# A layer norm whose mean and 1/std are read by VectorE straight from one double PSUM bank, and a last norm whose second half is summed earlier

## The chip, the cores and the metric

The kernel runs on one core of one Trainium2 chip. The metric is the device time of one execution in microseconds (us); the figure that counts is the median of several runs. A core has five engines that run their own queues in order: TensorE (PE; its weight loads are listed as PEld), VectorE (DVE), ScalarE (ACT), GpSimd (POOL) and SyncE (SP), which here only issues DMA transfers. PSUM is the memory that TensorE writes its products to; SBUF is the working memory of all engines.

## The reference: what is computed

Two layers of an encoder work on 576 tokens together: 512 of a prompt and 64 of a running stream with caches. Each layer ends in two residual sums with a layer norm behind each:

```python
mix = jnp.concatenate([conv_out, attn_out], axis=-1) @ w_o
x = layer_norm(ALPHA * x + mix, ln1_g, ln1_b)
gate, up = jnp.split(x @ w_gate_up, 2, axis=-1)
ffn = (jax.nn.silu(gate) * up) @ w_down
x = layer_norm(ALPHA * x + ffn, ln2_g, ln2_b)
```

Here `layer_norm` takes mean and variance over the 1024 features of a token. So there are four such norms: after `w_o` and after `w_down` in layer 0, and the same two in layer 1. The last of them gives the output `y`.

## The kernel before

**Layout.** The features lie on the partitions: X is held as 8 blocks (`KD` = 8) of 128 features by 576 tokens, in fp32. The tokens are worked on in two halves of 288 (`H[0]`, `H[1]`, `HT` = 288). Each matrix product is made of three fp32r products, with every operand split into a high part (XH, whi, hh; written by ScalarE) and a low part (XL, wlo, hl; the difference, written by VectorE or GpSimd).

**Order of the work.** The program records every operation with a priority (`nc.prio`, set locally by `with at(...)`) and a planner then places them on the engines one by one, by its own costs, by the priorities and by when buffers come free. That is why all operations carry one line number in the profile, L362, where the planner issues them. A buffer that is used in turn (`IN_TURN`) passes to its next user when its last reader is planned. The pool `pw` has one such buffer, tag "w": two PSUM banks of 512 fp32 columns, which the function `wide` hands out. The stats, the spreads, the convolution and others all take it in turn.

**A norm.** `residual` makes the product that is added to X, one block m of 128 features after the other: five blocks one by one, then the last three (m = 5, 6, 7) together, first the three of token half 0, then the three of half 1 (`order="last"`). For each block and half `take` adds the product to X (VectorE, "X<-X,prod") and `Sums.add` adds x and x squared to the running sums s1 and s2: ScalarE squares (tile sq), GpSimd adds, and VectorE adds for the very last block (`eng`, argument `last`). When block 7 of a half is summed, `Sums.norm` runs for that half:

- `Moments.stats`: six small matmuls with a column of ones give the sums over the partitions (tile stats, in the wide buffer), then six small operations on 96 x 3 numbers (five on VectorE, the square root on ScalarE) give minus mean and 1/std (tile st).
- `Moments.spread(0)` and `spread(1)`: three matmuls each against the identity bring minus mean, then 1/std, to all 128 partitions (tile spread, in the wide buffer), and ScalarE copies each to SBUF (tiles nmu and rstd). The second spread needs the wide buffer that the first copy frees.
- For the 8 blocks: add nmu, multiply by rstd (VectorE, "X<-X,nmu" and "X<-X,rstd"), gain and offset (ScalarE, "X<-X,prm"), and then XH (ScalarE) and XL (VectorE) for the next products; in the last norm a DMA to `y` instead.

The priorities of half 0's last takes and norm lie below those of half 1 by 300, so half 0's norm comes first.

Of the kernel before, what the change touches and what calls it, by code (L numbers as in the profile page):

```python
# [17 lines left out]
P = 128  # L18
D = 1024
KD = D // P  # L20
# [3 lines left out]
HT = T // 2  # L24
# [341 lines left out]
def stream_step(ctx, tc, ins, outs):  # L366
    ctx.enter_context(tc.nc.allow_low_precision(reason="float32r parts"))
    nc = Plan(tc)
# [16 lines left out]
    ident = const.tile([P, P], F32, name="ident")  # L385
# [4 lines left out]
    H = (slice(0, HT), slice(HT, T))  # L390
# [12 lines left out]
    def f(x):  # L403
        return x.bitcast(F32)
# [3 lines left out]
    def bank(name, tag="b"):  # L408
        return pb.tile([P, 512], F32, tag=tag, name=name, bufs=BANKS[tag])

    def wide(name):
        return pw.tile([P, 2, 512], F32, tag="w", name=name)
# [8 lines left out]
    def tmp(name, tag, n=T, bufs=2):  # L421
        return work.tile([P, n], F32, tag=tag, name=name, bufs=bufs)

    def probs(name):
        return tmp(name, "r", T, 3)
# [17 lines left out]
    def weight(src, n):  # L443

        raw = wp.tile([P, KD * P], F32, tag="raw", name="raw", bufs=2)
        hi = wp.tile([P, KD * P], F32R, tag="whi", name="whi")
        lo = wp.tile([P, KD * P], F32R, tag="wlo", name="wlo")
        nc.sync.dma_start(raw[:, :n], src)
        nc.scalar.activation(hi[:, :n], raw[:, :n], AF.Copy)
        nc.either.tensor_sub(lo[:, :n], raw[:, :n], f(hi[:, :n]))  # L450
        return hi, lo
# [74 lines left out]
    class Sums:  # L526
# [2 lines left out]
            self.s1 = slot.tile([P, UW], F32, tag="u0", name="s1")[:, :T]  # L529
            self.s2 = slot.tile([P, UW], F32, tag="u1", name="s2")[:, :T]  # L530

        def add(self, m, h, last=False):
            x = X[:, m, H[h]]
            a, b = self.s1[:, H[h]], self.s2[:, H[h]]
            if m == 0:
                ps = bank("shift")
                nc.tensor.matmul(ps[:, :HT], ones, x, start=True, stop=True)
                nc.vector.scalar_tensor_tensor(x, ps[:, :HT], -1.0 / P, x, op0=OP.mult, op1=OP.add)
                if h == 0:
                    self.c = slot.tile([P, UW], F32, tag="u2", name="shift")[:, :T]  # L540
                nc.scalar.activation(self.c[:, H[h]], ps[:, :HT], AF.Copy, scale=-1.0 / P)
                nc.gpsimd.tensor_copy(a, x)
                nc.scalar.activation(b, x, AF.Square)
                return
            eng = nc.vector if last else nc.gpsimd
            sq = probs("sq")[:, :HT]
            nc.scalar.activation(sq, x, AF.Square)
            eng.tensor_add(a, a, x)
            eng.tensor_add(b, b, sq)

        def norm(self, prm, og, ob, h, last):
            x = lambda k: X[:, k, H[h]]
            nmu, rstd = dst = [tmp(x, x, HT, n) for x, n in (("nmu", 1), ("rstd", 2))]
            mo = Moments(self.s1[:, H[h]], self.s2[:, H[h]], D, HT, 3, dst)
            mo.stats()
            mo.spread(0)
            mo.spread(1)
            for k in range(KD):
                nc.vector.tensor_add(x(k), x(k), nmu)
                nc.vector.tensor_mul(x(k), x(k), rstd)  # L560
                nc.scalar.activation(x(k), x(k), AF.Identity, scale=prm[:, og + k:og + k + 1],
                                     bias=prm[:, ob + k:ob + k + 1])
                if last:
                    nc.sync.dma_start(outs["y"][:, k, H[h]], x(k))
                else:
                    nc.scalar.activation(XH[:, k, H[h]], x(k), AF.Copy)
                    nc.vector.tensor_sub(XL[:, k, H[h]], x(k), f(XH[:, k, H[h]]))

    def residual(prm, wsrc, nk, rhs, og, ob, alpha, last=False):

        s = Sums()

        def take(m, h, ps):
            x = X[:, m, H[h]]
            if m == 0:
                nc.vector.scalar_tensor_tensor(x, x, alpha, ps[:, :HT], op0=OP.mult, op1=OP.add)
            else:
                nc.vector.scalar_tensor_tensor(x, x, alpha, s.c[:, H[h]], op0=OP.mult, op1=OP.add)
                nc.vector.tensor_add(x, x, ps[:, :HT])
            s.add(m, h, m == KD - 1)  # L580

        for m in range(KD - 3):
            out = products([weight(wsrc[m], nk * P)], rhs)[0]
            for h in range(2):
                take(m, h, out[h])
        ws = [weight(wsrc[m], nk * P) for m in range(KD - 3, KD)]
        urgent = nc.prio - 3000
        warm = small.tile([P, 1], F32, tag="warm", name="warm", bufs=2)
        for k in (nk // 2 - 1, nk - 1):
            nc.scalar.activation(warm, f(rhs[k][0][:, T - 1:T]), AF.Sqrt, bias=ones[:, 0:1], scale=0.0)  # L590

        def finish(i, h, ps):
            with at(urgent + 300 * h + 50 * i):
                take(KD - 3 + i, h, ps)
                if i == 2:
                    s.norm(prm, og, ob, h, last)

        products(ws, rhs, "last", take=finish)
# [728 lines left out]
```

## Time and profile before

| | |
|---|---|
| runs, us | 1522.31, 1516.83, 1520.78 (median 1520.78) |
| the profiled execution, us | 1524.12, with a span of 1522.4 from first to last instruction |
| mean granted TensorE clock | 0.939 of full speed |
| busy, share of the span | PE 95%, PEld 93%, DVE 73%, ACT 47%, POOL 33% |
| the chain that ended last | PE 78%, DVE 13%, ACT 3%, issue 2%, DMA 2% |

Busy times are sums over stages with different limits. In the product stages TensorE is at 100%; a norm is a place where the others decide when TensorE goes on. [...]

### The profile page before, as it was taken

How to read it: one execution, taken by the hardware profiler on the slowest of the kernel's cores; microseconds unless marked ns; L12 is line 12 of the kernel's file. 1: busy time of each engine (PE TensorE's matmuls, PEld its weight loads, DVE VectorE, ACT ScalarE, POOL GpSimd, SP SyncE). 2: the span in 40 equal slices, each digit the busy share in tenths (PEclk: the TensorE clock that was granted, in tenths of full speed). 3: DMA queues.
4: the chain of work that ended last, by engine and by line, in shares of the span. 5: the costliest groups of instructions: out<-in, count | busy, mean ns of one | idle time of the engine just before them, and what ended most of it. 6: DMA issues, size and time to landing. Idle time of an engine off the chain costs nothing.

```text
span 1522.4 us, 26598 instructions
## 1 busy us (share of the span) xinstructions
PE 1449.1 (95%) x10246; PEld 1413.3 (93%) x10246; DVE 1104.6 (73%) x2040; ACT 721.4 (47%) x1421; POOL 496.0 (33%) x437
## 2 busy tenths in 40 slices
PE   6999999998999999999998998999899999999996
PEld 6889897997999999999998998889889999999996
DVE  3679886468678577587768997855596875865875
ACT  4444445645446245265444434465363552543643
POOL 2322554243113123033614245633420230320342
PEclk9989787898999999999999995959999999999997
DMA  5614220011222322223234241101112222222221
GB/s 201 188 52 119 54 70 17 29 56 56 77 104 78 103 89 92 84 98 103 69 102 125 86 125 52 45 14 42 56 50 88 99 94 87 94 91 81 80 74 63
DMA packets 66207, 125.12 MB, mean 82 GB/s; under 512 B 27936, under 2 KB 34208, under 8 KB 66080
## 3 DMA queue, kind: packets, MB, share of 16 engines
q1 hardware_dynamic: 66080, 123.42, 25.3%
q8 instruction: 80, 1.31, 0.4%
q14 instruction: 47, 0.39, 0.1%
HBM read 108.81 MB, written 9.21 MB: 78 GB/s over the span
## 4 chain that ended last, share of the span: by engine, by line
PE 78%; DVE 13%; ACT 3%; issue 2%; DMA 2%; POOL 1%; SPq 1%; ACTq 0%; DVEq 0%; POOLq 0%
PE prod L362 33%; PE q L362 16%; PE r L362 8%; PE conv L362 5%; PE c L362 4%; PE po L362 3%; DVE X L362 2%; DVE sel L362 2%; DVE rope_h L362 2%; PE qk L362 2%; PE dots L362 2%; PE pp L362 2%; PE spread L362 2%; DVE wlo L362 2%; PE stats L362 1%
## 5 line engine op out<-in xcount | busy, mean ns | idle before, releaser
L362 DVE TENSOR_TENSOR wlo<-raw,whi 128x512 fp32r<-128x512 f32 (+2 forms) x199 | 246.2, 1239 | 90.8 <-ACT whi L362 88.7
L362 ACT ACTIVATE whi<-raw 128x1024 fp32r<-128x1024 f32 (+2 forms) x206 | 182.9, 889 | 254.5 <-PE prod L362 179.1
L362 PE MATMUL prod<-XH,whi 128*128 128x288 f32 (+2 forms) x928 | 282.9, 310 | 18.5 <-ACT whi L362 16.4
L362 PE MATMUL prod<-XH,wlo 128*128 128x288 f32 (+2 forms) x928 | 285.0, 310 | 7.4 <-DVE wlo L362 7.4
L362 PE MATMUL prod<-XL,whi 128*128 128x288 f32 (+2 forms) x928 | 285.9, 310 | 2.9 <-DVE XL L362 2.8
L362 PE MATMUL prod<-hl,whi 128*128 128x288 f32 x704 | 208.1, 296 | 0.7 <-DVE hl L362 0.5
L362 PE MATMUL prod<-hh,wlo 128*128 128x288 f32 x704 | 207.8, 296 | 0.0
L362 PE MATMUL prod<-hh,whi 128*128 128x288 f32 x704 | 207.0, 295 | 0.0
L362 PEld LDWEIGHTS prod<-XH,whi 128*128 128x128 f32 (+1 forms) x928 | 177.6, 193 | 22.5 <-ACT whi L362 17.3
L362 PEld LDWEIGHTS prod<-XH,wlo 128*128 128x128 f32 (+1 forms) x928 | 177.9, 192 | 10.4 <-DVE wlo L362 8.3
L362 PEld LDWEIGHTS prod<-XL,whi 128*128 128x128 f32 (+1 forms) x928 | 178.9, 193 | 7.7 <-DVE XL L362 5.8
L362 ACT ACTIVATE whi<-s 128x512 fp32r<-128x512 f32 x160 | 96.4, 626 | 134.9 <-PE q L362 102.0
L362 DVE TENSOR_TENSOR wlo<-s,whi 128x512 fp32r<-128x512 f32 x158 | 107.7, 703 | 63.5 <-ACT whi L362 62.5
L362 PE MATMUL q<-XH,wlo 128*128 128x288 f32 x480 | 141.2, 296 | 1.5 <-DVE wlo L362 1.3
L362 PE MATMUL q<-XL,whi 128*128 128x288 f32 x480 | 141.4, 295 | 0.0
L362 PE MATMUL q<-XH,whi 128*128 128x288 f32 x480 | 141.3, 295 | 0.0
L362 PEld LDWEIGHTS prod<-hl,whi 128*128 128x128 f32 x704 | 132.1, 188 | 1.8 <-DVE hl L362 1.4
L362 PEld LDWEIGHTS prod<-hh,wlo 128*128 128x128 f32 x704 | 132.0, 188 | 0.1
L362 PEld LDWEIGHTS prod<-hh,whi 128*128 128x128 f32 x704 | 131.9, 188 | 0.2
L362 POOL TENSOR_TENSOR s<-raw 128x512 f32<-128x512 f32 x28 | 45.0, 1611 | 247.8 <-DVE wlo L362 209.7
L362 DVE TENSOR_TENSOR X<-X,prod 128x288 f32<-128x288 f32 x120 | 53.4, 451 | 86.8 <-PE prod L362 86.1
L362 POOL TENSOR_TENSOR taps<-eyes,wv 128x640 f32<-128x640 f32 x64 | 86.9, 1361 | 71.0 <-PE conv L362 57.2
(197 smaller groups left out, 3560.1 us busy)
## 6 DMA issues: line engine op xcount, KB each, us to landing
raw<-in_w_u SPq DMA_DIRECT2D x44, 512.0 KB, 3.2
raw<-in_w_g SPq DMA_DIRECT2D x44, 512.0 KB, 3.2
raw<-in_w_in SPq DMA_DIRECT2D x36, 512.0 KB, 3.9
raw<-in_w_d SPq DMA_DIRECT2D x48, 384.0 KB, 3.0
raw<-in_w_o SPq DMA_DIRECT2D x16, 512.0 KB, 3.3
raw<-in_w_d SPq DMA_DIRECT2D x16, 256.0 KB, 2.6
rope_s<-rope_h SPq DMA_DIRECT2D x48, 72.0 KB, 2.0
ud<-u SPq DMA_DIRECT2D x8, 320.0 KB, 2.9
```

The costliest lines, as they stand in the source:

```text
L362: getattr(engine, op.method)(*map(take, op.args), **{k: take(v) for k, v in op.kw.items()})
```

## The change

`norm` no longer copies: both spreads go into one wide buffer, minus mean into bank 0 and 1/std into bank 1, and VectorE's adds and multiplications read them there. The buffer is held until half 0's last multiplication. `norm` gets a priority of its own, 125 above that of the half's takes. In the last norm alone, the takes of half 1 get the priority of those of half 0, ahead of half 0's norm, and block 6 of half 1 is summed by VectorE too.

```diff
-        def add(self, m, h, last=False):
+        def add(self, m, h, by_vector=False):
...
-            eng = nc.vector if last else nc.gpsimd
+            eng = nc.vector if by_vector else nc.gpsimd
...
         def norm(self, prm, og, ob, h, last):
             x = lambda k: X[:, k, H[h]]
-            nmu, rstd = dst = [tmp(x, x, HT, n) for x, n in (("nmu", 1), ("rstd", 2))]
-            mo = Moments(self.s1[:, H[h]], self.s2[:, H[h]], D, HT, 3, dst)
+            mo = Moments(self.s1[:, H[h]], self.s2[:, H[h]], D, HT, 3, None)
             mo.stats()
-            mo.spread(0)
-            mo.spread(1)
+            ps = wide("spread")
+            for b in range(2):
+                for i in range(3):
+                    nc.tensor.matmul(ps[:, b, i * mo.m:(i + 1) * mo.m],
+                                     mo.st[:mo.m, b, i:i + 1].to_broadcast([mo.m, P]), ident[:mo.m, :mo.m],
+                                     start=True, stop=True)
+            nmu, rstd = ps[:, 0, :HT], ps[:, 1, :HT]
...
-            s.add(m, h, m == KD - 1)
+            s.add(m, h, m >= KD - 1 - (last and h))
...
-            with at(urgent + 300 * h + 50 * i):
+            with at(urgent + (-300 if last else 300) * h + 50 * i):
                 take(KD - 3 + i, h, ps)
+            with at(urgent + 300 * h + 125):
                 if i == 2:
                     s.norm(prm, og, ob, h, last)
```

The planner makes an order of its own from this. The rows below are of the built programs; "waits" names the engines whose semaphores the instruction waits for, and a row with xN stands for N equal instructions.

TensorE, last norm, half 0, before: from the first spread to the second (spread writes minus mean, then 1/std; prod is block 5 of half 1).

```order
L362 MATMUL spread<-ident,st 128x96 [waits DVE_49]
L362 MATMUL spread<-ident,st 128x96 x2
L362 MATMUL prod<-hh_15247,whi 128x288
L362 MATMUL prod<-hl_15261,whi 128x288
L362 MATMUL prod<-hh_15247,wlo 128x288
L362 MATMUL prod<-hh_15386,whi 128x288
L362 MATMUL prod<-hl_15400,whi 128x288
L362 MATMUL prod<-hh_15386,wlo 128x288
L362 MATMUL spread<-ident,st 128x96 [waits DVE_49,Activation_49]
L362 MATMUL spread<-ident,st 128x96 x2
```

The same place in the changed program.

```order
L362 MATMUL spread<-ident,st 128x96 [waits DVE_49]
L362 MATMUL spread<-ident,st 128x96 x2
L362 MATMUL prod<-hh_15217,whi 128x288
L362 MATMUL prod<-hl_15231,whi 128x288
L362 MATMUL prod<-hh_15217,wlo 128x288
L362 MATMUL spread<-ident,st 128x96 [waits DVE_49]
L362 MATMUL spread<-ident,st 128x96
L362 MATMUL spread<-ident,st 128x96 [waits DVE_49]
L362 MATMUL prod<-hh_15356,whi 128x288
```

Three products fewer stand between the spreads, and the second spread is cut: it has a wait for VectorE ahead of its first and ahead of its third matmul.

VectorE, last norm, half 0's norm and what follows to half 1's stats, before (X<-X,prod are the takes of half 1's blocks 6 and 7, s_15953 and s_15951 its s1 and s2).

```order
L362 TENSOR_TENSOR X<-X,nmu 128x288 [waits Activation_49]
L362 TENSOR_TENSOR X<-X,nmu 128x288 x3
L362 TENSOR_TENSOR X<-X,rstd 128x288 [waits DVE_49,Activation_49]
L362 TENSOR_TENSOR X<-X,rstd 128x288 [waits DVE_49] x3
L362 TENSOR_TENSOR X<-X,nmu 128x288 x2
L362 TENSOR_TENSOR X<-X,rstd 128x288 [waits DVE_49] x2
L362 TENSOR_TENSOR X<-X,prod 128x288 [waits PE_49] x2
L362 TENSOR_TENSOR s_15953<-s_15953,X 128x288 [waits DVE_49,Pool_49]
L362 TENSOR_TENSOR s_15951<-s_15951,sq 128x288 [waits Activation_49,Pool_49]
L362 TENSOR_SCALAR st<-stats 96x3 [waits PE_49]
```

(The pair of rows for two adds and two multiplications stands twice in the program.) The same place in the changed program; the spread operand is minus mean or 1/std.

```order
L362 TENSOR_TENSOR X<-X,spread 128x288 [waits PE_49] x3
L362 TENSOR_TENSOR X<-X,spread 128x288 [waits DVE_49] x3
L362 TENSOR_TENSOR X<-X,spread 128x288 x2
L362 TENSOR_TENSOR X<-X,prod 128x288 [waits PE_49]
L362 TENSOR_TENSOR X<-X,spread 128x288 [waits DVE_49]
L362 TENSOR_TENSOR s_15923<-s_15923,X 128x288 [waits DVE_49,Pool_49]
L362 TENSOR_TENSOR s_15921<-s_15921,sq 128x288 [waits Activation_49,Pool_49]
L362 TENSOR_TENSOR X<-X,spread 128x288 x2
L362 TENSOR_TENSOR X<-X,prod 128x288 [waits PE_49]
L362 TENSOR_TENSOR s_15923<-s_15923,X 128x288 [waits DVE_49]
L362 TENSOR_TENSOR X<-X,spread 128x288 [waits DVE_49] x2
L362 TENSOR_SCALAR st<-stats 96x3 [waits PE_49]
```

(Three rows of the same kinds are left out ahead of the last two.) The first three adds each wait for TensorE; half 1's takes and sums now stand between half 0's adds and multiplications, and the last multiplications of half 0 come right ahead of half 1's statistics, whose first matmul on TensorE waits for them.

TensorE, norm after `w_o` of layer 0, half 1, in the changed program, from the first spread on (prod is now the first product of the feed-forward part).

```order
L362 MATMUL prod<-XL,whi 128x288
L362 MATMUL spread<-ident,st 128x96 [waits DVE_49,PE_49]
L362 MATMUL spread<-ident,st 128x96 x2
L362 MATMUL prod<-XH,wlo 128x288
L362 MATMUL spread<-ident,st 128x96 [waits DVE_49] x2
L362 MATMUL spread<-ident,st 128x96
```

Before, six products stood between the two spreads of that half; here it is one, and the second spread waits for VectorE ahead of its first and its second matmul. In layer 1 the attention's and the convolution's instructions also stand in another order, on all engines: a planner that works from start to end carries any difference on. On TensorE 623 of 9559 instructions stand in other places by a comparison of the two orders, most of them between layer 0's last norm and layer 1's attention.

## Rows read from the trace of the kernel before

**Rows 1.** The profile's page: busy time of each engine, and the granted clock in 40 slices of the span.

```profile
PE 1449.1 (95%) x10246; PEld 1413.3 (93%) x10246; DVE 1104.6 (73%) x2040; ACT 721.4 (47%) x1421; POOL 496.0 (33%) x437
PEclk9989787898999999999999995959999999999997
```

**Rows 2.** The timeline of the last norm from 1497.4 us, VectorE: start, duration, operation, count, idle time before it and what ended it.

```profile
1496.98 0.45 DVE L362 TENSOR_TENSOR X<-X,prod 128x288 f32<-128x288 f32 x1 [0.28 <-PE prod L362]
1498.07 2.28 DVE L362 TENSOR_TENSOR X<-X,nmu 128x288 f32<-128x288 f32 x4 [0.55 <-ACT nmu L362]
...
1503.96 0.82 DVE L362 TENSOR_TENSOR X<-X,rstd 128x288 f32<-128x288 f32 x2
1504.70 0.81 DVE L362 TENSOR_TENSOR X<-X,prod 128x288 f32<-128x288 f32 x2
1506.12 1.05 DVE L362 TENSOR_TENSOR s<-s,X 128x288 f32<-128x288 f32 x1 [0.61 <-POOL s L362]
...
1512.16 1.56 DVE L362 TENSOR_TENSOR X<-X,nmu 128x288 f32<-128x288 f32 x4 [1.55 <-ACT nmu L362]
1514.26 1.56 DVE L362 TENSOR_TENSOR X<-X,rstd 128x288 f32<-128x288 f32 x4 [0.53 <-ACT rstd L362]
...
1517.94 0.83 DVE L362 TENSOR_TENSOR X<-X,rstd 128x288 f32<-128x288 f32 x2
```

**Rows 3.** The same stretch on TensorE and ScalarE: the spreads and their copies in half 0, the last product, and half 1's stats and spreads (a matmul of fp32 is two passes, so x6 are three).

```profile
1496.78 0.81 PE L362 MATMUL spread<-ident,st 96*128 96x96 f32 x6
1497.63 0.41 ACT L362 ACTIVATE nmu<-spread 128x288 f32<-128x288 f32 x1 [0.69 <-PE spread L362]
1498.25 0.81 PE L362 MATMUL spread<-ident,st 96*128 96x96 f32 x6
1502.78 0.29 PE L362 MATMUL prod<-hh,wlo 128*128 128x288 f32 x1
1507.32 1.09 PE L362 MATMUL stats<-ones,s 128*96 128x1 f32 x6 [4.25 <-DVE s L362]
1508.66 1.12 PE L362 MATMUL stats<-ones,s 128*96 128x1 f32 x6 [0.25 <-DVE st L362]
1510.03 1.59 PE L362 MATMUL spread<-ident,st 96*128 96x96 f32 x6 [0.25 <-DVE st L362]
1512.18 1.59 PE L362 MATMUL spread<-ident,st 96*128 96x96 f32 x6 [0.56 <-ACT nmu L362]
1518.44 1.14 ACT L362 ACTIVATE X<-X,prm 128x288 f32<-128x288 f32 x2 [0.33 <-DVE X L362]
```

**Rows 4.** All instructions that write X on VectorE: duration in ns, least/median/most.

```profile
L362 DVE TENSOR_TENSOR X<-X,prod x120: 438/454/464, 293.9 to 1505.1; 128x288 f32<-128x288 f32 x120
L362 DVE TENSOR_TENSOR X<-X,nmu x64: 445/454/1052, 335.0 to 1517.6; 128x288 f32<-128x288 f32 x64
L362 DVE TENSOR_TENSOR X<-X,rstd x64: 445/454/485, 336.8 to 1518.3; 128x288 f32<-128x288 f32 x64
```

**Rows 5.** ScalarE's copies of a spread: duration in ns, least/median/most, of all eight halves.

```profile
L362 ACT ACTIVATE nmu<-spread x8: 388/412/413, 334.5 to 1511.7; 128x288 f32<-128x288 f32 x8
```

**Rows 6.** TensorE's idle times of 0.25 us or more in and behind the norms after `w_o` (layer 0, then layer 1), from its timeline.

```profile
346.19 0.61 PE L362 MATMUL prod<-XH,wlo 128*128 128x288 f32 x1 [3.55 <-DVE wlo L362]
348.00 1.09 PE L362 MATMUL stats<-ones,s 128*96 128x1 f32 x6 [0.48 <-DVE s L362]
368.97 0.40 PE L362 MATMUL prod<-XL,whi 128*128 128x288 f32 x1 [0.56 <-DVE XL L362]
...
1094.92 0.40 PE L362 MATMUL prod<-XH,wlo 128*128 128x288 f32 x1 [3.55 <-DVE wlo L362]
1117.71 0.40 PE L362 MATMUL prod<-XL,whi 128*128 128x288 f32 x1 [0.56 <-DVE XL L362]
```

**Rows 7.** Windows around those two idle times and around the last norm, and around a stall in layer 1's attention: length, TensorE's busy time and instructions, granted clock, DMA.

```profile
346.00:359.00 13.00, 12.33 (x55) 0.50 0.22 82
1096.00:1106.00 10.00, 9.26 (x44) 0.52 0.27 101
1503.00:1506.00 3.00, 0.08 (x1) 0.99 0.70 231
1506.00:1510.00 4.00, 2.21 (x12) 0.50 0.21 69
917.00:944.00 27.00, 25.01 (x117) 0.50 0.14 41
```

**Rows 8.** TensorE's timeline in the norm after `w_down` of layer 0: the spreads, and the idle times beside them.

```profile
751.62 0.81 PE L362 MATMUL spread<-ident,st 96*128 96x96 f32 x6
755.72 0.67 PE L362 MATMUL prod<-XH,whi 128*128 128x288 f32 x3 [0.87 <-ACT XH L362]
768.27 0.81 PE L362 MATMUL spread<-ident,st 96*128 96x96 f32 x6
```

**Rows 9.** TensorE's longest idle time in layer 1's attention.

```profile
916.30 0.66 PE L362 MATMUL qk<-k,q 128*128 128x128 f32 x2 [3.48 <-DVE mx L362]
```

## The prediction

> **What bounds the kernel now.** I read the page first: TensorE is busy for 95% of the span, VectorE for 73%, ScalarE for 47% [rows 1]. So work taken off ScalarE or VectorE is worth something only where TensorE stands still, and the row of granted clocks has three dents beside its end [rows 1]. The places that the change touches were then read from TensorE's timeline and from windows around its idle times. The last norm [rows 2, 3]: half 0's first spread ends at 1496.78 + 0.81 = 1497.59, ScalarE copies it from 1497.63, VectorE adds from 1498.07. The last product ends at 1502.78 + 0.29 = 1503.07, and TensorE then waits 4.25 us until half 1's sums are there (1507.32). From there nothing covers anything: stats, spread, copy, adds, spread, copy, multiplications, each behind the one before, all at a granted clock of 0.50 [rows 7], and the last multiplication ends at 1517.94 + 0.83 = 1518.77. The norms behind `w_o` each hold an idle time of 3.55 us that VectorE's wlo ends, and shorter ones [rows 6]; behind the long one the clock stands at 0.50 or 0.52 for 13 and 10 us [rows 7]. In the norm behind layer 0's `w_down` the only idle time near the spreads is 0.87 us [rows 8].
>
> **What is removed.** Sixteen copies on ScalarE, 412 ns each [rows 5], are 6.6 us of an engine that is busy for half of the span: nothing by itself. What counts is the delay of one copy ahead of the first add (1497.63 to 1498.07, 0.44 us), and of a second ahead of the multiplications in half 1. If only this happened, half 0 of the last norm would begin 0.44 us earlier and half 1 would end 2 x 0.44 = 0.9 us earlier.
>
> **What VectorE pays for reading PSUM.** The trace has that very shape: X plus a product in PSUM takes 438/454/464 ns (120 of them), X plus nmu in SBUF 445/454/1052, X times rstd 445/454/485 [rows 4]. Same median. So 128 operations cost between 128 x (438 - 454) = -2.0 us and 128 x (464 - 454) = +1.3 us of VectorE's time, and I take nothing. A small gain speaks from the one slow group: the first four adds of half 0 took 2.28 us where four others took 1.56 [rows 2], so that 0.7 us hung on something that readers of SBUF met there; adds that read PSUM may lose it. [...]
>
> **The hidden wait.** The wide buffer is one tile, and the built program orders its users as a whole: a matmul that writes bank 1 waits for an add that only reads bank 0, and the next add waits for that matmul. This is to be seen in the rows of order in the section on the change. In half 0 the order becomes add 0, two matmuls of the second spread, add 1, the third matmul, add 2. In half 1 (and where the first matmul goes ahead of add 0) it is add 0, two matmuls, add 1. TensorE works in order, so it stands still behind each such wait, and every product behind it too.
>
> **Last norm, half 0.** A release takes about 0.04 us (1497.59 to 1497.63), a matmul of a spread 0.81 / 3 = 0.27 at full clock [rows 3], a VectorE operation 0.45, and in a row one each (1.56 - 0.45) / 3 = 0.37 [rows 2]. Add 0 from 1497.63 to 1498.08; two matmuls to 1498.66; add 1 from 1498.70 to 1499.15; third matmul to 1499.46; add 2 from 1499.50. The 0.44 that the copy gave back is gone by then, and more. Up to half 0's last multiplication there are 22 VectorE operations (16 of the norm, two takes, four sums, two of these formerly GpSimd's); 20 from add 2 on are 19 x 0.37 + 0.45 = 7.48, to 1506.98. The 0.61 us that VectorE waited for GpSimd's sum [rows 2] goes. Stats need the buffer, free at 1506.98, and begin some 0.15 later, as before behind the sum (1506.12 + 1.05 to 1507.32): 1507.13, or 0.2 earlier. TensorE loses about 0.20 ahead of the second spread (three products end at 1497.59 + 0.33, add 0 at 1498.08 and a release) and 0.53 ahead of its third matmul: the last product ends near 1503.8. This is hidden, as VectorE reaches block 7's take about 1505.
>
> **Last norm, half 1.** Stats to first spread took 1510.03 - 1507.32 = 2.71 [rows 3], so it runs from 1509.84 to 1511.43 (1.59). First matmul of the second, 1.59 / 3 = 0.53, to 1511.96; add 0 to 1512.45; two matmuls to 1513.55; add 1 from 1513.59; 15 operations, 14 x 0.37 + 0.45 = 5.63, to 1519.22. That is +0.45 against 1518.77; ScalarE's gain and the output's transfer follow as before (rows 3's last). In half 1 the copies' 0.9 us are paid back by matmuls that now stand ahead of add 1. I take **+0.5**. [...] Upper bound: sums that wait for a square or a take, +1.3.
>
> **Norms behind `w_o`.** TensorE's two new waits (0.2 + 0.53) fall into the time before 346.19 and 1094.92, and shorten the 3.55 us there, as the end of that is set by VectorE's queue: half 0's norm, then XL, then wlo. That queue loses the waits ahead of add 1 and add 2 (1498.70 - 1498.08 and 1499.50 - 1499.15: 0.62 + 0.35 us) and gains the 0.44 of the copy and up to 0.7 of the slow adds: wlo comes between 0.2 earlier and 0.5 later. In half 1 TensorE has one new wait of about 0.55 (add 0 and two releases), and the norm starts earlier against the idle of 0.56 before an XL [rows 6], which may take part of it. I take **+0.5** for each of the two, with -0.6 and +1.3 as ends.
>
> **Norm behind layer 0's `w_down`.** No long idle time covers it. New waits of 0.73 in half 0 and 0.55 in half 1, 1.3 in all, against 0.87 us of idle time [rows 8] that they may fall into: between 0.4 and 1.3, I take **+0.8**.
>
> **The rest of the order.** Layer 1's attention and convolution come out in another order, since their pieces are planned among the changed norms. Their cost can't be summed. The nearest rows: a stall of 3.48 us behind VectorE's mx [rows 9], and the 27 us at a clock of 0.50 behind it, with 25 us of TensorE's work in them [rows 7], which at full clock would be half, some 12.5 less. Such a place may vanish or another may arise; I take **0**, and -4 to +4 for small shifts.
>
> **Sum.** 0.5 + 2 x 0.5 + 0.8 + 0 = +2.3 with all taken at their middle; the possible shortening of the slow adds in four half 0s is worth some 0.5 less where it lies on a path, which makes +1.8. The profiled execution took 1524.12, so 1525.9 for such a one; it stands 3.3 above the runs' median of 1520.78, against which the forecast is **1522.5**. I count 0.5%, 7.6 us, as the least that a measurement of this kernel can tell: below 1513.2 is faster, above 1528.4 slower.
>
> **Rivals.**
> 1. *The change does only what it says.* If the waits on the whole tile fall where the engines wait anyway, the last norm gives 0.44 + 0.9 less, four other halves up to 0.44 each: -1 to -5, **1518**. For it: the removed idle on GpSimd. Against: the order of VectorE's first adds shows the waits. Chance 0.18.
> 2. *A half-clock stretch goes, faster.* If TensorE's idle time of 3.55 us shrinks enough for the clock to stay at 1.00, the 13 us at 0.50 and 10 us at 0.52 [rows 7] give back up to 12.33 / 2 + 9.26 / 2 = 10.8 us; or the 27 us of layer 1's attention give 12.5. One of them: **1512**. Against: the idle time is ended by VectorE's queue, which is hardly shorter. Chance 0.13.
> 3. *A new stall in layer 1's attention, slower.* The reordered softmax makes TensorE wait once more as at 916.3, 3.5 us, and a stretch as that of 27 us follows at half clock: 3.5 + 12.5 = 16 at most, half of it for a shorter stretch, **1531**. It decides from a wait of about the 3.5 us that rows 9 show. For it: 623 instructions of TensorE move, and the stall of before hangs on a maximum on VectorE that is queued among others. Against: the existing stall already has its place, and one may as well go. Chance 0.13.
> 4. *PSUM reads cost more than SBUF reads*, by the 0.01 us of rows 4's upper end or a little more: 32 on the last norm's path, +0.3 and up, **1523**. [...] Chance 0.03, and inside the forecast's own range.
>
> My forecast keeps 0.53, with a range of its own of 1518 to 1527. Cases 1 and 4 and it lie within 0.5%: 0.74; faster 0.13, slower 0.13. Eight in ten lie between **1514** and **1529**, halfway into rivals 2 and 3.
>
> **What would show it.** In the trace after: VectorE's adds and multiplications from the spread at a median of 454 ns (clearly more: rival 4). TensorE's idle times released by VectorE's X inside the second spreads, 0.2 and 0.5 us in half 0; without them, rival 1. In the last norm, the second add 1.0 us after the first, the last product near 0.7 us later, the idle time ahead of half 1's stats near 3.3 in place of 4.25 us, and the clock still 0.50 there. Stretches at 0.50 behind the `w_o` norms of the same length (shorter: rival 2), and the attention of layer 1 with as much time at half clock as before (more: rival 3). The prediction is wrong if half-clock time anywhere changes by over 10 us, for everything else in the sum is smaller than that.

## The result, and the profile of the changed kernel

The changed kernel takes **1528.07 us** in the median against 1517.56 us before (with more runs of the kernel before than were known at the time of the prediction). The ratio is 1.0066, with a 95% interval of 1.0044 to 1.0087: slower, by about 10 us. Medians are of all executions, while ratios and their intervals, here and below, leave out executions that took over 1.5% more than the fastest of the same kernel.

The two profiled executions do not show that at first sight: 1523.01 us after, 1524.12 us before. The page of the changed kernel, with the rows that answer to [rows 1]:

```profile
PE 1441.5 (95%) x10246; PEld 1404.8 (92%) x10246; DVE 1102.2 (72%) x2039; ACT 715.0 (47%) x1405; POOL 499.4 (33%) x438
PEclk9999797898999999999998996979999999999998
```

The mean clock is 0.947 over a span of 1521.2 us, where the execution before had 0.939. Since the granted clock of these traces is either 1.00 or 0.50, that is 2 x (1 - 0.947) x 1521.2 = 161 us at half clock against 2 x (1 - 0.939) x 1522.4 = 186 us before. These 25 us fewer are worth up to 12 us, and they can't be put down to the change. Most of them lie between half 1's statistics behind `w_down` and layer 1's norm behind `w_o`, where the clock was 0.88 before and 0.91 after; but there it was 0.89 in a second execution of the changed kernel, and 0.91 in `prio_again` below, whose order on TensorE is that of before. The stretch from the convolution's statistics in layer 0 to the first norm, which the change does not touch, took 83.4 us in this execution before, 82.0 after, and 77.4 to 84.3 in the executions further below. So a single pair of executions has to be compared stage by stage. This table does it by the starts of the statistics' matmuls (us; "half 0 to 1" is from one half's statistics to the other's):

| stretch | before | changed | changed, again |
|---|---|---|---|
| layer 0, norm behind `w_o`, half 0 to 1 | 16.5 | 17.3 | 17.3 |
| layer 0, from there through the feed-forward part | 398.4 | 401.7 | 402.4 |
| norm behind `w_down`, with layer 1's start and attention, to the convolution's statistics | 249.9 | 249.9 | 251.6 |
| layer 1, norm behind `w_o`, half 0 to 1 | 16.5 | 17.2 | 17.3 |
| layer 1, from there through the feed-forward part | 397.9 | 399.7 | 400.3 |
| last norm, half 0 to 1 | 12.7 | 12.8 | 12.8 |
| last norm, half 1 | 15.0 | 14.9 | 14.9 |

Left out are the way to the first norm (331.5, 327.0 and 326.9 us) and layer 1's stretch from the convolution's statistics to its norm (84.0, 80.7 and 84.1 us; 77.8 to 84.1 in all executions below, in the old order and in the new). Summed over the table, the changed kernel's two executions lie 6.6 and 9.7 us above. Most of it stands in the feed-forward stretches, in which the change edits nothing. In windows (length, TensorE's busy time and instructions, granted clock, DMA), before and then after:

```profile
348.00:746.37 398.37, 393.82 (x2906) 0.99 0.26 89
1096.74:1494.60 397.86, 394.66 (x2906) 0.98 0.24 82
```

```profile
344.31:745.98 401.67, 395.10 (x2905) 0.98 0.27 89
1093.79:1493.46 399.67, 393.54 (x2905) 0.99 0.25 82
```

Length less busy time is TensorE's idle time: it grew by 2.0 us in layer 0 and by 2.9 in layer 1. The rest is a difference of busy time (+1.3 and -1.1 us), which depends on the clock: a spread's six passes take 0.81 us at 1.00 and 1.59 us at 0.50 [rows 3].

**What was changed by hand behaves about as forecast.** VectorE's reads of PSUM, least/median/most in ns, against [rows 4]:

```profile
L362 DVE TENSOR_TENSOR X<-X,spread x128: 420/448/455, 330.0 to 1517.2; 128x288 f32<-128x288 f32 x128
```

They cost no more than reads of SBUF: 448 ns in the median, for 454 before. The slow add of [rows 2] is gone: it was the second of the first four, 1.05 us long from 1498.56, beside a sum of GpSimd's (0.85 us from 1498.45). Here the first add, 0.46 us from 1496.48, runs beside such a sum of 0.80 us from 1496.37, and neither is slowed. The last norm, VectorE and then TensorE, as in [rows 2, 3]:

```profile
1496.48 0.46 DVE L362 TENSOR_TENSOR X<-X,spread 128x288 f32<-128x288 f32 x1
1497.72 0.45 DVE L362 TENSOR_TENSOR X<-X,spread 128x288 f32<-128x288 f32 x1 [0.78 <-PE spread L362]
1498.72 2.28 DVE L362 TENSOR_TENSOR X<-X,spread 128x288 f32<-128x288 f32 x6 [0.55 <-PE spread L362]
...
1512.08 5.56 DVE L362 TENSOR_TENSOR X<-X,spread 128x288 f32<-128x288 f32 x15 [1.26 <-PE spread L362]
```

```profile
1496.99 0.69 PE L362 MATMUL spread<-ident,st 96*128 96x96 f32 x4
1498.22 0.46 PE L362 MATMUL spread<-ident,st 96*128 96x96 f32 x2 [0.55 <-DVE X L362]
...
1502.81 0.29 PE L362 MATMUL prod<-hh,wlo 128*128 128x288 f32 x1
1506.30 1.30 PE L362 MATMUL stats<-ones,s 128*96 128x1 f32 x12 [3.20 <-DVE X L362]
1508.33 2.00 PE L362 MATMUL spread<-ident,st 96*128 96x96 f32 x8 [0.73 <-DVE st L362]
1510.87 1.17 PE L362 MATMUL spread<-ident,st 96*128 96x96 f32 x4 [0.55 <-DVE X L362]
```

The hidden wait, by which the engines wait for the double bank as a whole, is there: VectorE's second add waits 0.78 us for TensorE, TensorE 0.55 us for the add, VectorE 0.55 us for TensorE again. In layer 0's norm behind `w_o`, which answers to the first rows of [rows 6]:

```profile
331.78 0.46 PE L362 MATMUL spread<-ident,st 96*128 96x96 f32 x2 [0.55 <-DVE X L362]
341.07 0.40 PE L362 MATMUL prod<-XH,whi 128*128 128x288 f32 x1 [1.61 <-ACT whi L362]
343.18 0.61 PE L362 MATMUL prod<-XH,wlo 128*128 128x288 f32 x1 [1.57 <-DVE wlo L362]
352.36 1.17 PE L362 MATMUL spread<-ident,st 96*128 96x96 f32 x4 [0.55 <-DVE X L362]
```

**Where the feed-forward part loses it.** Some 15 to 35 us behind half 1's statistics stand the sums of X that the feed-forward part needs (tiles t, t2l, t3l, t4l), and some 40 us behind the statistics the first products from these (tile q; pc is ScalarE's copy of one). VectorE, GpSimd and TensorE there before:

```profile
373.97 0.76 DVE L362 TENSOR_TENSOR t2l<-t,t2h 128x576 fp32r<-128x576 f32 x1
374.64 0.76 DVE L362 TENSOR_TENSOR t3l<-t,t3h 128x576 fp32r<-128x576 f32 x1
375.31 0.46 DVE L362 TENSOR_TENSOR t4l<-t,t4h 128x288 fp32r<-128x288 f32 x1
...
374.62 1.81 POOL L362 TENSOR_TENSOR t4l<-t,t4h 128x288 fp32r<-128x288 f32 x1 [23.90 <-ACT t4h L362]
...
388.35 0.40 PE L362 MATMUL q<-t2h,whi 128*128 128x288 f32 x1 [0.95 <-ACT pc L362]
```

The same place in the changed kernel:

```profile
369.81 0.45 DVE L362 TENSOR_TENSOR sg<-prod,sg 128x288 f32<-128x288 f32 x1
370.18 2.59 DVE L362 TENSOR_TENSOR t<-X,t 128x576 f32<-128x576 f32 x1
372.69 1.84 DVE L362 TENSOR_TENSOR t2l<-t,t2h 128x576 fp32r<-128x576 f32 x1
374.46 1.84 DVE L362 TENSOR_TENSOR t3l<-t,t3h 128x576 fp32r<-128x576 f32 x1
376.22 3.00 DVE L362 TENSOR_TENSOR t4l<-t,t4h 128x288 fp32r<-128x288 f32 x2
...
367.83 4.33 POOL L362 TENSOR_TENSOR wlo<-raw,whi 128x1024 fp32r<-128x1024 f32 x1 [22.60 <-ACT whi L362]
372.12 1.80 POOL L362 TENSOR_TENSOR s<-raw 128x512 f32<-128x512 f32 x1
373.89 1.80 POOL L362 TENSOR_TENSOR s<-s,raw 128x512 f32<-128x512 f32 x1
...
381.75 0.40 PE L362 MATMUL q<-XH,wlo 128*128 128x288 f32 x1 [1.14 <-DVE wlo L362]
387.23 0.40 PE L362 MATMUL q<-t2h,whi 128*128 128x288 f32 x1 [2.31 <-ACT pc L362]
```

Before, GpSimd had been idle for 23.9 us. Now the planner, which may put a wlo or an s (sums of weights) on either engine, gives one wlo and several s to GpSimd right beside VectorE's operations on t. These have two operands in SBUF, and each takes 2.4 to 3.4 times as long: 1.84 for 0.76, 2.59 for 0.76, 3.00 for two of 0.46. Everything behind them on VectorE is late, and TensorE waits 1.14 us for wlo and 2.31 us for pc, where before it waited 0.95 us for pc. Behind the wait of 2.31 us the granted clock is 0.50 from 387.6 to 391.0; before, it stays at 1.00 there.

### The profile page after: what moved, and what is told of

Same layout as the page of the kernel before. It is cut to its first block, busy times and chain, and to the rows that moved or that the text cites. A ratio compares the mean times of both kernels' runs of the same rounds, so it can differ in the third digit from the quotient of the medians.

```text
span 1521.2 us, 26581 instructions
## 1 busy us (share of the span) xinstructions
PE 1441.5 (95%) x10246; PEld 1404.8 (92%) x10246; DVE 1102.2 (72%) x2039; ACT 715.0 (47%) x1405; POOL 499.4 (33%) x438
## 4 chain that ended last, share of the span: by engine, by line
PE 78%; DVE 15%; ACT 2%; DMA 2%; issue 2%; SPq 1%; POOL 0%; ACTq 0%; DVEq 0%; POOLq 0%
PE prod L362 33%; PE q L362 16%; PE r L362 8%; PE conv L362 5%; PE c L362 4%; PE po L362 3%; DVE X L362 3%; DVE sel L362 2%; PE spread L362 2%; DVE wlo L362 2%; PE qk L362 2%; PE dots L362 2%; DVE rope_h L362 2%; PE pp L362 2%; DVE XL L362 1%
## 5 line engine op out<-in xcount | busy, mean ns | idle before, releaser
L362 DVE TENSOR_TENSOR wlo<-raw,whi 128x1024 fp32r<-128x1024 f32 (+3 forms) x196 | 237.0, 1210 | 93.7 <-ACT whi L362 91.6
```

The lines of the kernel that those rows point to most:

```text
L362: getattr(engine, op.method)(*map(take, op.args), **{k: take(v) for k, v in op.kw.items()})
```

## The experiments

**Is it the priorities?** The changed kernel once more, then each half of the change alone: `psum_only` reads mean and 1/std from PSUM with the old priorities, `prio_only` has the new priorities and sums with the old copies.

> The changed kernel unaltered, beside the kernel before on the same chip. Its profiled execution took 1523.01 us, but the median of its runs is 1528.07 against 1517.56 before. If the difference is made of TensorE's idle time (79.7 us in the trace of the changed kernel, 73.3 before, so 6.4 more) the ratio repeats at about 1.005 to 1.007, and spans at an equal mean clock differ by 6 to 8 us. If it is made of half-clock stretches that come and go, the ratio moves towards 1.000 and only the clock tells the runs apart.

```diff
 # psum_only, against the changed kernel
-            s.add(m, h, m >= KD - 1 - (last and h))
+            s.add(m, h, m == KD - 1)
...
-            with at(urgent + (-300 if last else 300) * h + 50 * i):
+            with at(urgent + 300 * h + 50 * i):
                 take(KD - 3 + i, h, ps)
-            with at(urgent + 300 * h + 125):
                 if i == 2:
                     s.norm(prm, og, ob, h, last)
```

> Mean and 1/std read from the double bank, but priorities and the last norm's sums as in the kernel before. The order on TensorE is that of the changed kernel in every row, VectorE's differs in the last norm alone. Theories A and B: as slow as the changed kernel, ratio 1.005 to 1.008, a little slower by up to 0.6 us for the GpSimd sum that the last norm waits for again. Theory C (priorities are the cause): ratio 1.000.

`prio_only` makes the opposite edit in the kernel before.

> The copies on ScalarE kept, only the priorities and the last norm's sums changed. TensorE's order is that of the kernel before in every row; VectorE's differs in the last norm alone. Theories A and B: ratio 1.000, or some 0.5 us faster, since VectorE no longer waits 0.61 us for GpSimd's sum in the last norm. Theory C: ratio 1.005 to 1.007.

Measured, on one chip: the changed kernel 1531.26 us, ratio to before 1.0101 (1.0051 to 1.0150); `psum_only` 1534.01 us, 1.0101 (1.0061 to 1.0142); `prio_only` 1512.91 us, 0.9986 (0.9961 to 1.0011). The slowdown repeats, and it belongs to reading PSUM with the buffer held, not to the priorities.

**Is it the wait on the whole tile?** In `gather` the order of the changed kernel is kept, but the six matmuls stand together ahead of the first add.

```diff
-            for op in self.schedule():
+            for op in self.together(self.schedule()):
...
+    def together(self, order):
+        late = {id(op): op for six in self.sixes for op in six[3:]}
+        behind = {id(six[2]): six[3:] for six in self.sixes}
+        out = []
+        for op in order:
+            if id(op) not in late:
+                out += [op] + behind.get(id(op), [])
+        return out
```

> The order of the changed kernel, with one thing moved: in every norm the three matmuls of 1/std stand directly behind the three of minus mean on TensorE, ahead of the first add. Theory A (the waits on the whole tile cost the time): the idle times of 0.26 and 0.55 us ahead of a spread's matmuls go, 0.8 us in half 0 and 0.55 in half 1 with what follows them, 5 us or more in all: about 1522, ratio to before near 1.003. Theory B (the new order that a longer hold of the wide buffer gives the rest of the program costs the time): at most 2 us less than the changed kernel, ratio 1.005 to 1.007.

1522.75 us, ratio 1.0056 (1.0031 to 1.0082). In this kernel some halves spread 1/std ahead of its reciprocal, so the numbers that it normalises with differ, while instructions and their count don't. `gather2` puts the three late matmuls behind the reciprocal too (`behind` the later of the third matmul and the reciprocal).

> As the kernel that put the six matmuls together, but now behind the reciprocal as well, so that 1/std is final when it is spread. Theory A's share alone: the idle times of 0.26 and 0.55 us ahead of the spreads go. Expected 3 to 5 us below the changed kernel, ratio to before 1.004 to 1.006; the feed-forward stretches stay at 400 to 402 us if theory B is right.

1523.62 us, ratio 1.0039 (1.0009 to 1.0068). From half 0's to half 1's statistics behind `w_o` it takes 16.4 us in both layers where the changed kernel takes 17.3 and 17.2, and in the last norm 12.2 for 12.8. So in these three norms the waits cost some 0.6 to 0.9 us, about as priced; behind `w_down` nothing is won (17.4 us between the statistics, where the changed kernel takes 17.1). The feed-forward stretches stay long, at 399.5 and 401.1 us. Theory A holds a part, B the larger one.

**Is it the order?** Two kernels exchange data path and order. `old_plan` lets the planner work on the kernel before and then issues that order without the copies, with both spreads in one double bank and their six matmuls together behind the reciprocal:

```diff
+                if id(op) in self.copies:
+                    continue
                 for t in op.tiles.values():
+                    if t.ap is None and id(t) in self.alias:
+                        base, part = self.alias[id(t)]
+                        t.ap = part(base.ap)
...
+            nc.copies |= {id(ops[3]), id(ops[7])}
+            nc.alias[id(p1)] = p0, lambda ap: ap[:, 1:2, :]
+            nc.alias[id(nmu.tile)] = p0, lambda ap: ap[:, 0, :HT]
+            nc.alias[id(rstd.tile)] = p0, lambda ap: ap[:, 1, :HT]
```

> The planner works on the kernel before, with its copies; when its order is issued, the copies are left out, both spreads go into one double bank, the six matmuls stand together (behind the reciprocal, so that no add stands between them), and VectorE reads the bank. So VectorE reads PSUM and the buffer is held, but the order on TensorE is that of before except for the moved spreads. Theory B (the new order costs most): the feed-forward stretch from half 1's statistics to the next norm takes 397 to 398.5 us as before (400 to 402 in the changed kernel), ratio to before 0.998 to 1.002. Theory A' (reading PSUM or holding the buffer costs the time wherever the rest stands): ratio 1.005 or more.

`new_plan_copies` issues the changed kernel's order, with a copy behind each three matmuls, which the adds and multiplications read:

```diff
+            sb = {}
+            def copy(b):
+                def emit(eng, op):
+                    sb[b] = work.pool.tile([P, HT], F32, tag=("nmu.0", "rstd.0")[b], name=("nmu", "rstd")[b], bufs=1)
+                    eng.scalar.activation(sb[b], ps.tile.ap[:, b, :HT], AF.Copy)
+                return emit
...
+            for b in range(2):
+                nc.copied[id(nc.ops[-4 + 3 * b])] = copy(b)
+            nmu, rstd = (View(ps.tile, v.part, v.idx, lambda b=b: sb[b]) for b, v in
+                         enumerate((ps[:, 0, :HT], ps[:, 1, :HT])))
```

> The converse: order, engines and priorities of the changed kernel on every engine, but ScalarE copies mean and 1/std behind each three matmuls to SBUF and VectorE's adds and multiplications read them there. Theory B: the feed-forward stretches stay at 400 to 402 us, ratio to before 1.004 to 1.008. Theory A (waits on the whole tile between VectorE and TensorE): those stretches and the ratio come back to 397 to 398.5 us and 0.998 to 1.002.

`old_plan`: 1523.27 us, ratio 1.0042 (1.0008 to 1.0076), above its expectation. `new_plan_copies`: 1525.96 us, 1.0059 (1.0031 to 1.0088). The feed-forward stretches, `old_plan` first (in the profiled execution of `new_plan_copies` the stretch with layer 1's attention took 281.9 us, so it is read only elsewhere):

```profile
351.88:749.73 397.85, 393.57 (x2907) 0.99 0.28 90
1102.74:1499.97 397.23, 393.45 (x2906) 0.99 0.26 83
```

```profile
347.74:747.47 399.73, 393.26 (x2904) 0.99 0.28 89
1124.08:1524.28 400.20, 395.27 (x2904) 0.98 0.25 82
```

The stretches go with the order, not with who reads PSUM: 397 to 398 in the old order, 400 in the new one even with the copies. What `old_plan` loses stands elsewhere: from half 0's to half 1's statistics behind `w_o` 18.7 us where before it was 16.5, since TensorE now waits longer for the wlo of [rows 6]. VectorE's last operations up to that wlo, before and then in `old_plan`, with TensorE's wait:

```profile
342.69 0.84 DVE L362 TENSOR_TENSOR XL<-X,XH 128x288 fp32r<-128x288 f32 x2
...
344.16 0.84 DVE L362 TENSOR_TENSOR XL<-X,XH 128x288 fp32r<-128x288 f32 x2
344.90 1.23 DVE L362 TENSOR_TENSOR wlo<-raw,whi 128x1024 fp32r<-128x1024 f32 x1
```

```profile
344.53 1.43 DVE L380 TENSOR_TENSOR XL<-X,XH 128x288 fp32r<-128x288 f32 x2
...
346.61 1.94 DVE L380 TENSOR_TENSOR XL<-X,XH 128x288 fp32r<-128x288 f32 x2
348.47 1.80 DVE L380 TENSOR_TENSOR wlo<-raw,whi 128x1024 fp32r<-128x1024 f32 x1
...
350.33 0.61 PE L380 MATMUL prod<-XH,wlo 128*128 128x288 f32 x1 [6.02 <-DVE wlo L380]
```

So the old order with PSUM reads isn't free either: 6.02 us in place of 3.55, in each of the two layers. The rows divide the 2.5 us: 0.23 from a first add that comes later behind six matmuls than it did behind three and a copy (1.33 us after the reciprocal's start, for 1.10), and 0.59 + 1.10 + 0.57 from three operations with two operands in SBUF that take longer, two pairs of XL and the wlo. GpSimd's sums s stand beside them. Before, it was GpSimd that lost there: two sums took 3.91 us, which alone take 0.81 each. Why they get in earlier in `old_plan` is not shown.

**Is it GpSimd beside VectorE?** `on_vector` keeps order and data path of the changed kernel and only takes the subtractions and additions that the planner gave to GpSimd beside the sums of X to VectorE, at the same place of the order:

```diff
+    def on_vector(self, order):
+        for ops in self.preludes:
+            at = [order.index(op) for op in ops]
+            for op in order[min(at):max(at) + 12]:
+                if len(op.engines) > 1 and op.done[2] == "gpsimd":
+                    op.done = (*op.done[:2], "vector")
```

> Order and data path of the changed kernel; five or six subtractions per layer that its planner gave to GpSimd, at the sums of X ahead of the feed-forward part, go to VectorE at the same place of the order. Theory D (VectorE's operations with two SBUF inputs are slowed while GpSimd reads SBUF: t2l, t3l and t4l take 1.84 and 1.54 us instead of 0.76 and 0.46, and TensorE then waits 1.14 us for wlo and 2.31 us for pc): t2l, t3l, t4l return to 0.76 and 0.46 us, and the feed-forward stretches get 2 to 4 us shorter each, ratio to before 1.001 to 1.005. Without it VectorE only gets some 4 us more to do there: the stretches get 2 to 4 us longer each.

1522.14 us, ratio 1.0030 (0.9997 to 1.0063); this interval overlaps that of the changed kernel, so what the edit does is read from the stretches. VectorE has more to do there and is done sooner: t2l and t3l are back at 0.76 us, t4l at 0.46, and both stretches are as short as before.

```profile
L371 DVE TENSOR_TENSOR t2l<-t,t2h x4: 753/764/767, 363.9 to 1116.5; 128x576 fp32r<-128x576 f32 x4
...
383.41 0.40 PE L371 MATMUL q<-t2h,whi 128*128 128x288 f32 x1 [1.30 <-ACT pc L371]
...
344.17:741.50 397.33, 391.66 (x2904) 0.99 0.28 90
1088.05:1485.45 397.40, 393.47 (x2904) 0.98 0.26 83
```

The wait for pc fell from 2.31 to 1.30 us, and the one of 1.14 us for wlo is gone.

`lock_added` asks from the other side, with the kernel before and idle work for GpSimd at the same place:

```diff
+    def load(eng, op):
...
+        for i in range(8):
+            eng.gpsimd.tensor_add(out, op.args[0].real()[:, 0, :256] if i == 0 else cos.real()[:, :256], sin.real()[:, :256])
...
                 nc.vector.tensor_sub(t2, b(1, 1), t1)
+                if k == 0:
+                    nc.extra[id(nc.ops[-1])] = load
```

> The kernel before with every instruction in its order, and eight additions of 256 columns from SBUF more on GpSimd in each layer, at the sums of X ahead of the feed-forward part, where GpSimd otherwise idles for 23.9 us; their result is read by nobody. Theory D: VectorE's t and t2l, t3l, t4l operations beside them take up to 1.8 us instead of 0.76, and the feed-forward stretches get 1 to 3 us longer each; ratio to before 1.001 to 1.004. Without it: those operations stay at 0.76 us and the stretches at 397 to 398.5 us.

1528.27 us, ratio 1.0115 (1.0065 to 1.0165): more than expected, and in another way.

```profile
362.82 10.11 POOL L400 TENSOR_TENSOR spare<-t,sin 128x256 f32<-128x256 f32 x1 [15.53 <-DVE t L362]
373.01 6.87 POOL L400 TENSOR_TENSOR spare<-cos,sin 128x256 f32<-128x256 f32 x7
...
372.26 0.82 DVE L362 TENSOR_TENSOR sg<-prod,sg 128x288 f32<-128x288 f32 x2
...
383.55 0.40 PE L362 MATMUL q<-XH,whi 128*128 128x288 f32 x1 [1.37 <-ACT whi L362]
385.94 0.61 PE L362 MATMUL q<-XH,wlo 128*128 128x288 f32 x1 [1.85 <-DVE wlo L362]
...
344.57:749.52 404.95, 397.96 (x2906) 0.98 0.28 88
1112.45:1516.77 404.32, 397.95 (x2907) 0.98 0.26 81
```

Here it is GpSimd that is held. Its first addition of 256 columns takes 10.11 us (10.12 in layer 1; the shortest of the others take 0.73), seven others together 6.87; VectorE's sums stay at 0.76 us. The addition comes to its end as VectorE reaches sg, whose one operand lies in PSUM. GpSimd's own sums of weights are then late, TensorE waits for the whi and wlo made of them, and both stretches are 6.5 us longer than before; 2.4 and 3.2 us of this are idle time of TensorE, the rest is busy time, which goes with the clock (0.98 in both, for 0.99 and 0.98 before). The expectation had the sufferer wrong, the place and the sign right. That also reads the changed kernel's rows anew: its wlo on GpSimd took 4.33 us, and VectorE's first slow operation (2.59 us, from 370.18) comes right behind an sg too. From there the starts alternate (372.12 GpSimd, 372.69 VectorE, 373.89 GpSimd, 374.46 VectorE), which reads as the two engines taking turns: 1.84 us would be VectorE's own 0.76 and 1.08 of waiting.

Both engines lose in these rows. VectorE takes 1.84 for 0.76 us in the changed kernel, where its slow operation of 370.18 starts while GpSimd's wlo is under way (367.83 to 372.16). GpSimd takes 10.11 us here, where its addition of 362.82 starts while VectorE's t is under way (362.66 to 363.42). What decides which of the two waits is not shown: VectorE's t of 369.14 in the changed kernel also starts beside that wlo, and takes 0.75 us.

**Do these two parts make the whole?** `mended` is the changed kernel with both mends, those of `gather2` and `on_vector`.

> The changed kernel with both mends: the six matmuls of a norm together, and GpSimd's subtractions at the sums of X on VectorE. If waits and slowed VectorE operations are the two largest parts, the ratio to before is 1.000 to 1.003, with feed-forward stretches of 397 to 398 us, 16.4 to 16.6 us between the halves' statistics behind w_o, and only layer 1's attention (some 2 to 3 us) above before. If something else carries the time: 1.004 or more.

1515.07 us, ratio 1.0001 (0.9969 to 1.0033), feed-forward stretches of 397.15 and 396.53 us, 16.4 us between the statistics behind `w_o`. With both, nothing is left of the slowdown that this measurement can tell from zero; the interval leaves room for some 5 us either way. (The mends were timed on another chip than `again`, each beside the kernel before on its own chip.)

**Is a part of the change worth keeping?** `prio_again` repeats `prio_only`; `prio_vector` adds to it the edit of `on_vector`.

> The copies kept, the priorities and the last norm's sums of the change, and the same subtractions on VectorE instead of GpSimd. In the kernel before they run behind the sums of X and slow little: within 1 us of the kernel with priorities alone, either way; ratio to before 0.996 to 1.000.

> The copies kept, only the priorities and the last norm's sums changed, once more. From half 1's statistics to those of the last norm's end its trace was 10.31 us between the two halves' statistics against 12.72 before, so 2.4 us: ratio 0.9975 to 0.9995.

`prio_vector`: 1516.65 us, 1.0002 (0.9968 to 1.0037), no gain. Its median lies 7 us above that of `prio_again`, where 1 us was expected, but the intervals overlap, and its feed-forward stretches of 397.5 and 397.9 us are within 1 us of those of `prio_again` (397.6 and 397.2). `prio_again`: 1509.48 us, 0.9979 (0.9956 to 1.0003). The last norm from half 0's to half 1's statistics, `prio_again`, then the kernel before:

```profile
1477.10:1487.42 10.32, 8.46 (x69) 1.00 0.18 60
```

```profile
1494.60:1507.32 12.72, 8.48 (x69) 0.94 0.29 94
```

These 2.4 us are there in all three kernels that have the new priorities and the copies of before (10.31, 10.32 and 10.32 us), and 2.4 us are 0.16%: the two ratios, 0.9986 and 0.9979, lie beside it, though each interval still holds 1. The changed kernel has the same priorities and takes 12.84 us: half 1's statistics wait there for half 0's last multiplication, which holds the wide buffer. With the copies put back into the changed order (`new_plan_copies`) it is 10.7 us. So the change gives back what its priorities gain. `prio_only`, which is also `prio_again`, is the fastest kernel of this study, by a margin that is shown in its trace and not by its times alone.

## Why the prediction was right in its range and wrong in its likeliest case

The measured 1528.07 us lies inside 1514 to 1529, near its upper end, but the likeliest case was +1.7 us with 0.74 on "within 0.5%", and it is 0.66% (0.44 to 0.87). That the range holds it is luck: its upper end was set halfway into rival 3, a new stall in layer 1's attention, and most of the loss came from somewhere else and by another mechanism.

- **VectorE reading PSUM: right.** Median 448 ns; rival 4 is out. The spreads' 128 reads take 420/448/455 ns from PSUM, where the reads of nmu and rstd took 445/454 in the least and the median from SBUF [rows 4].
- **The hidden wait: right**, in place and size: 0.55 us where 0.53 was worked out, and 0.26 behind `w_o` where 0.20 was; rival 1 falls. Its matmuls were mis-sized: the two take 0.69 us, not 0.54, and the lone third 0.46, not 0.27, so that add 2 comes 2.24 us behind add 0, not 1.87.
- **Last norm: +0.5 forecast, about 0.0 measured** (27.77 us from half 0's statistics to the end against 27.75). TensorE idles 3.20 us ahead of the statistics, as forecast (3.3), but the twelve passes then ran in 1.30 us, where before they took 1.09 + 1.12 us [rows 3]: the granted clock was 0.82 over them (1.00 in the first 0.8 us), where before it was 0.50.
- **Norms behind `w_o`: +0.5 forecast, +0.8 and +0.7 measured.** The 3.55 us became 1.61 for whi and 1.57 for wlo. Half 1's wait of 0.55 us lies in the feed-forward stretches of the table.
- **Norm behind `w_down`: +0.8 forecast.** The two waits of 0.55 us are there, but the planner also moved 19 of TensorE's instructions behind it, so that only the sum with layer 1's attention can be compared: 249.9 and 251.6 us against 249.9 (and 248.5 to 250.2 in four other executions in the old order, but 262.3 in that of `lock_added`). In the new order five other executions range from 248.8 to 255.6, and that of `new_plan_copies` took 281.9. That part of the new order may cost 2 to 3 us, but stalls and half-clock time differ by more than that between executions of one order, and no experiment separates it.
- **"The rest of the order ... I take 0, and -4 to +4": this step failed.** It looked for the reordering where most rows move, in layer 1's attention and convolution, and rival 3 sought the slower case there, too. The larger cost lies in the beginnings of the two feed-forward parts, whose stretches are +3.3 and +1.8 us in this execution and +4.0 and +2.4 in the second, and of a kind that the sum had no term for: GpSimd working beside VectorE. The rows of GpSimd's order, in which a wlo now stands beside the sums of X, were not read. The 0.7 us of the slow add among the first four in [rows 2] was a sign of it: one VectorE operation with two SBUF operands at 1.05 us beside others at 0.45 [rows 4]. It was booked as a small gain for the operations that stop reading SBUF, and not asked of those that still do.
- **The sign of half-clock time: of no use as set.** "Wrong if half-clock time anywhere changes by over 10 us" was met in layer 1 (clock 0.88 to 0.91 over some 315 us), but executions of one order differ there by as much, so it says nothing for or against.

Why the planner puts that wlo on GpSimd in the changed kernel is not settled. It follows from the PSUM reads with the held buffer, since `psum_only` has the same order on TensorE and `prio_only` that of before; the planner prices an operation for each engine by itself, mostly by its columns, whatever the other engine does (`price` in the kernel).

## What to carry to other kernels

A planner that is handed a small edit answers with a new order far from it: compare the order of every engine, GpSimd's too, and ask of each instruction that comes to stand beside others whether the two share something. Where a kernel splits work over VectorE and GpSimd, price operations with two SBUF operands on the one and SBUF reads on the other as if only one of them could run at a time: side by side, 0.76 us became 1.84 on VectorE here, and 0.73 became 10.11 on GpSimd. And a tile of two banks that is written and read in turn was waited for as one in this program, 0.55 to 0.78 us each time in the last norm's half 0: put all writes ahead of the first read.

## What the runs showed of the hardware that was not expected

- VectorE, with two operands in SBUF, and GpSimd hold each other up, and either may be the loser: VectorE's 0.76 us became 1.84 in the changed kernel, GpSimd's addition of 256 columns became 10.11 us while VectorE issued operations with two SBUF operands one behind the other. In both layers that addition ended beside sg, VectorE's first operation with an operand in PSUM (10.11 and 10.12 us); that such an operation lets GpSimd in is read from these coincidences, not tested.
- Stretches at half clock come and go between executions of the same order: the stretch from layer 0's convolution statistics to the first norm took 77.4 us at a granted clock of 0.89 (`psum_only`), 83.4 at 0.83 (the kernel before) and 84.3 at 0.81 (`gather2`), with the same instructions. The difference is most of the whole effect's size, so stages had to be compared, not totals.
